# A macaron layer on one core: linear attention by 128-token tiles, the mixer's first products ahead of the last transposes, the result stored by column chunks

## The chip, the cores and the metric

The kernel runs on one core of one Trainium2 chip. Its engines work side by side, each through its own list of instructions in order: TensorE (PE in the rows) multiplies matrices, VectorE (DVE) and ScalarE (ACT) do elementwise work, GpSimd (POOL) does a little of it, and SyncE (SP) starts nearly all transfers between the chip's memory and the core's. An instruction that waits holds up everything behind it on its own engine. The metric is the device time of one execution in microseconds (us), the median over several; less is better. A matmul's weight load shows in the rows as an engine of its own, PEld.

## The reference

One decoder layer on 256 tokens of width 2048, in float32:

```python
h = h + 0.5 * swiglu(rmsnorm(h, ffn1_norm), ffn1_w_in, ffn1_w_out)      # inner width 5632
u = rmsnorm(h, mix_norm) @ w_in_mix       # pool input, q, k, v, output gate, gate's low rank (16)
y = concat(pool_mixer(u), gla_mixer(u))
h = h + y @ w_out_mix
h = h + 0.5 * swiglu(rmsnorm(h, ffn2_norm), ffn2_w_in, ffn2_w_out)
out = rmsnorm(h, final_norm)
```

The part `gla_mixer` is gated linear attention with 4 heads (keys of 128, values of 256), written in chunks of 64 tokens:

```python
b = cumsum(log_alpha) within a chunk           # log_alpha < 0, one per token and key column
q_dec, k_inv, k_tail = q * exp(b), k * exp(-b), k * exp(b_last - b)
o = (q_dec @ k_inv.T, kept where j <= i) @ v + q_dec @ state
state = state * exp(b_last) + k_tail.T @ v     # after each chunk
```

## The kernel before

**Tiles.** The 256 tokens are two tiles of 128 rows (`t` = 0 and 1; `h[0]` and `h[1]` show as `h_76` and `h_77` in listings). A product's columns go by chunks of `CW` = 512. Each float32 product is made of three passes in a rounded format (`three`, L162): high part by high part, high by low, low by high. ScalarE makes the high part of a weight block (`wh_...`, L108), VectorE the low part (`wl_...`, L109), in 14 buffers, that is seven pairs of high and low.

**Stages.** The order is FFN1 (`fi`, `fo`), mixer (`mgr`, `mk`, `mq`, `mv`, `mg`, `mp`, each a call of `project`), `w_out_mix` (`h`), FFN2 (`zi`, `zo`), final norm. The weights stream in through SyncE's queue, all in the order of their use. FFN products go by steps of two kinds listed in the table `OUT`: "S" is a plain step, "W" a step with fewer matmuls that first needs sums of weight blocks on VectorE and writes a second accumulator, `pw_...`.

**Accumulators.** The accumulator memory (PSUM) has 8 banks. In the FFNs two tags, `x` and `y`, of two two-bank buffers each hold a group's `ps_...` and `pw_...` in turn. In the mixer four banks (`ps_acc`) hold projections and four (`ps_t`) everything else. At each change of stage one set of pools closes and the next opens.

**FFN1's end.** `fo` is made for two column halves (`np_` = 0, 1). When a half is complete, `finish1` adds it to `h` (L561), sums squares (ScalarE) and transposes the new columns on TensorE (`transposed_rows`, 8 transposes `tp_h` for each chunk `n`, L367); ScalarE and VectorE turn each transposed tile into the high and low parts `h_hi`, `h_lo` (L286, L287), which are the moving operands of every mixer product. Chunks 0 and 1 are transposed in the middle of `np_` = 1, chunks 2 and 3 behind its last product. Then come the first halves (contraction over chunks 0 and 1) of `mgr` and `mk`, and then the second halves.

**Linear attention.** After q and k are projected, `bc` (L667) and `sf` (L676) are sums of the log decay by matmuls with a constant triangle, `sp` (L723) the scores of each 128-token tile (masked to 64-token blocks), `kv` (L744) the product of keys and values of each of the first three chunks, `st` the states (three, VectorE L749 and L754), `o` (L780, L785) the output: one matmul with the masked scores and, for each 64 rows behind the first chunk, one with a state.

**The end.** `finish2` adds the last half of `zo` to `h` (L915), finds the norm's factor `fin_r` (reduce and small steps on VectorE, a power on GpSimd L947, square sums on ScalarE), scales and stores the rows. GpSimd multiplies chunk 2 by the final gain (L924), VectorE does chunk 3 with gain and factor in two halves (L956) and scales chunks 1 and 2 by the factor (L966), ScalarE scales chunk 0.

The order on each engine is not written out by hand: a scheduler in the compiler's Tile layer sets it from the program's order, the buffers and its own costs.

## Time and profile before

| what | value |
|---|---|
| median of 3 runs | 1752.91 us (1752.67 to 1753.26) |
| the profiled execution | 1751.42 us |
| its span, first to last instruction | 1749.6 us |
| mean granted clock of TensorE | 0.996 |
| TensorE busy | 1726.8 us, 99% |
| VectorE busy | 1324.7 us, 76% |
| ScalarE busy | 912.3 us, 52% |
| weights and activations read | 334.56 MB |

The profile is one execution. Its span leaves 1.8 us of its time outside, and its time is 1.5 us under the median of the runs. Times in the rows count from the span's start. A row of the timeline gives the start, the time to the end of the last instruction that it merges, and in brackets how long the engine was idle before it and what ended that. Matmuls overlap, so one that shows 0.39 us may start 0.23 us after the one before; what a matmul costs is read from start to start. A plain float32 matmul shows as two records, one for each of its passes; a transpose shows as one.

### The profile page before, as it was taken

The numbers are of one execution on the slowest core, as the hardware profiler recorded it, in microseconds if no ns is written. First come the engines' busy times: TensorE is split into PE (matmuls) and PEld (weight loads), VectorE is DVE, ScalarE is ACT, GpSimd is POOL, SyncE is SP. The second block draws the span as 40 slices with busy tenths as digits, with TensorE's granted clock in tenths as the row PEclk, the third lists the DMA queues.
The fourth block names the chain that finished last, engine by engine and source line by source line (L and its number), as shares of the span: only waits on it lengthen the run. The fifth ranks groups of instructions, "written<-read, shape, count | busy, mean of one in ns | idle before, by whom it ended". The sixth has DMA issues, their size and how long they took to land.

```text
span 1749.6 us, 20543 instructions
## 1 busy us (share of the span) xinstructions
PE 1726.8 (99%) x7858; PEld 1428.2 (82%) x7858; DVE 1324.7 (76%) x1503; ACT 912.3 (52%) x1118; POOL 24.7 (1%) x26
## 2 busy tenths in 40 slices
PE   9999999999999999899999999999999999999997
PEld 6888888888888888788978888888888888888886
DVE  7978896878985878654555667878967788868788
ACT  8555544545544555464445554555545555545553
POOL 0000000000000000000000000000000000000002
PEclk9999999999999999999999999999999999999999
DMA  9564565655555655544554555654564645664652
GB/s 343 195 232 169 198 222 182 214 176 210 194 196 191 214 172 179 174 168 163 169 196 153 192 172 177 217 178 173 215 224 162 236 152 201 221 218 153 250 180 97
DMA packets 52052, 337.98 MB, mean 193 GB/s; under 512 B 5985, under 2 KB 9441, under 8 KB 13042
## 3 DMA queue, kind: packets, MB, share of 16 engines
q1 hardware_dynamic: 51522, 336.13, 55.0%
q8 instruction: 61, 1.00, 0.2%
q10 hardware_dynamic: 432, 0.55, 0.1%
q14 instruction: 37, 0.30, 0.0%
HBM read 334.56 MB, written 2.10 MB: 192 GB/s over the span
## 4 chain that ended last, share of the span: by engine, by line
PE 97%; DVE 1%; ACT 0%; DMA 0%; issue 0%; SPq 0%; POOL 0%; POOLq 0%; DVEq 0%; ACTq 0%
PE ps_zi L165 24%; PE ps_fi L165 23%; PE ps_zo L165 11%; PE ps_fo L165 11%; PE ps_h L165 5%; PE pw_fi L165 3%; PE pw_zi L165 3%; PE ps_mp L165 3%; PE ps_mv L165 2%; PE pw_fo L165 2%; PE pw_zo L165 2%; PE ps_mg L165 2%; PE ps_mk L165 1%; PE ps_mq L165 1%; PE ps_mgr L165 1%; PE ztp L441 1%
## 5 line engine op out<-in xcount | busy, mean ns | idle before, releaser
L109 DVE TENSOR_TENSOR wl_zi<-wr_zi,wh_zi 128x1024 fp32r<-128x1024 f32 (+1 forms) x216 | 250.6, 1173 | 106.7 <-ACT wh_zi L108 102.4
L108 ACT CAST wh_zi<-wr_zi 128x1024 fp32r<-128x1024 f32 (+1 forms) x216 | 215.7, 1012 | 217.9 <-PE ps_zi L165 150.8
L109 DVE TENSOR_TENSOR wl_fi<-wr_fi,wh_fi 128x1024 fp32r<-128x1024 f32 (+1 forms) x218 | 249.9, 1164 | 85.4 <-ACT wh_fi L108 81.1
L108 ACT CAST wh_fi<-wr_fi 128x1024 fp32r<-128x1024 f32 (+1 forms) x218 | 214.6, 1004 | 188.5 <-PE ps_fi L165 117.2
L165 PE MATMUL ps_fi<-wh_fi,xT_hi 128*128 128x512 f32 x584 | 226.8, 390 | 1.7 <-ACT wh_fi L108 1.7
L165 PE MATMUL ps_fi<-wl_fi,xT_hi 128*128 128x512 f32 x584 | 228.1, 391 | 0.1
L165 PE MATMUL ps_zi<-wl_zi,h_hi 128*128 128x512 f32 x584 | 228.0, 390 | 0.0
L165 PE MATMUL ps_zi<-wh_zi,h_hi 128*128 128x512 f32 x584 | 227.9, 390 | 0.0
L165 PE MATMUL ps_zi<-wh_zi,h_lo 128*128 128x512 f32 x584 | 227.6, 390 | 0.0
L165 PE MATMUL ps_fi<-wh_fi,xT_lo 128*128 128x512 f32 x584 | 226.4, 390 | 0.3 <-DVE xT_lo L287 0.3
L108 ACT CAST wh_fo<-wr_fo 128x1024 fp32r<-128x1024 f32 (+1 forms) x116 | 111.4, 999 | 94.3 <-DMA wr_fo<-in_ffn_w_out 35.1
L108 ACT CAST wh_zo<-wr_zo 128x1024 fp32r<-128x1024 f32 (+1 forms) x116 | 111.4, 998 | 92.7 <-DMA wr_zo<-in_ffn_w_out 34.1
L109 DVE TENSOR_TENSOR wl_fo<-wr_fo,wh_fo 128x1024 fp32r<-128x1024 f32 (+1 forms) x116 | 130.1, 1157 | 33.0 <-ACT wh_fo L108 32.7
L109 DVE TENSOR_TENSOR wl_zo<-wr_zo,wh_zo 128x1024 fp32r<-128x1024 f32 (+1 forms) x116 | 131.4, 1168 | 30.0 <-ACT wh_zo L108 25.2
L165 PEld LDWEIGHTS ps_fi<-wh_fi,xT_hi 128*128 128x128 f32 x584 | 109.5, 188 | 25.2 <-ACT wh_fi L108 2.8
L165 PEld LDWEIGHTS ps_fi<-wl_fi,xT_hi 128*128 128x128 f32 x584 | 109.6, 188 | 23.8 <-DVE wl_fi L109 1.4
L165 PEld LDWEIGHTS ps_fi<-wh_fi,xT_lo 128*128 128x128 f32 x584 | 109.6, 188 | 23.2 <-DVE xT_lo L287 0.7
L165 PEld LDWEIGHTS ps_zi<-wh_zi,h_lo 128*128 128x128 f32 x584 | 109.7, 188 | 22.5
L165 PEld LDWEIGHTS ps_zi<-wh_zi,h_hi 128*128 128x128 f32 x584 | 109.6, 188 | 22.5
L165 PEld LDWEIGHTS ps_zi<-wl_zi,h_hi 128*128 128x128 f32 x584 | 109.7, 188 | 22.3
L165 PE MATMUL ps_zo<-wl_zo,zhi 128*128 128x512 f32 (+1 forms) x272 | 105.2, 387 | 0.0
L165 PE MATMUL ps_zo<-wh_zo,zlo 128*128 128x512 f32 (+1 forms) x272 | 105.1, 386 | 0.0
(343 smaller groups left out, 3091.6 us busy)
## 6 DMA issues: line engine op xcount, KB each, us to landing
wr_zi<-in_ffn_w_in SPq DMA_DIRECT2D x88, 1024.0 KB, 4.9
wr_fi<-in_ffn_w_in SPq DMA_DIRECT2D x86, 1024.0 KB, 5.0
wr_fo<-in_ffn_w_out SPq DMA_DIRECT2D x44, 1024.0 KB, 5.1
wr_zo<-in_ffn_w_out SPq DMA_DIRECT2D x44, 1024.0 KB, 5.1
wr_h<-in_w_out_mix SPq DMA_DIRECT2D x16, 1024.0 KB, 5.0
wr_mv<-in_w_mv SPq DMA_DIRECT2D x8, 1024.0 KB, 4.9
wr_mp<-in_w_mp SPq DMA_DIRECT2D x8, 1024.0 KB, 4.9
wr_mg<-in_w_mg SPq DMA_DIRECT2D x8, 704.0 KB, 4.1
```

Of the source, the lines that this page charges most:

```text
L108: nc.scalar.copy(out=hi, in_=src)
L109: nc.vector.tensor_tensor(out=lo, in0=src, in1=hi.bitcast(F32), op=ALU.subtract)
L165: nc.tensor.matmul(ps, x, y, start=start and i == 0, stop=stop and i == 2, **kw)
L441: nc.tensor.transpose(tp[:, t, k, :], a_t[t][:, k * P : (k + 1) * P], ident)
```

## The change

- The `y` accumulators become a pool (`psy`) that lives through the whole kernel. `project` takes one two-bank pair of it in place of two single banks of `ps_acc`. FFN2 begins with `y`.
- `finish1` for the last half issues the first halves of `mgr` and `mk` between the updates of `h` and the last 16 transposes.
- In `OUT[3]`'s second list (the last slab of both FFNs' second products) the order S W S W S S becomes S S W W S S.
- Linear attention goes by tiles of 128 tokens. There is one state in place of three, so `sf`, `ktail`, `kv` and `st` are made for tile 0 alone, over 128 tokens; `o` takes the state only for tile 1, in one matmul of 128 rows. In return the scores between a tile's first and second 64 tokens (`sx`) are made, after VectorE has scaled the second half of `qdT`.
- At the end VectorE multiplies chunks 2 and 3 by gain and factor itself, GpSimd's two multiplications of the last half go, only tile 1 is worked in halves, and each chunk of 512 columns is stored by a transfer of its own (256 KB): chunks 2 and 3 on SyncE's queue, 0 and 1 on ScalarE's.

```diff
-        ((0, 0, "S"), (1, 0, "W"), (0, 1, "S"), (1, 1, "W"), (2, 0, "S"), (2, 1, "S")),
+        ((0, 0, "S"), (0, 1, "S"), (1, 0, "W"), (1, 1, "W"), (2, 0, "S"), (2, 1, "S")),
...
-        turn = [0]
+        turn = [0 if first else 1]
...
-    psum1 = ffn1.enter_context(tc.tile_pool(name="psum1", bufs=2, space=PSUM, reuse_waits="tile"))
+    psy = ctx.enter_context(tc.tile_pool(name="psy", bufs=2, space=PSUM))
+    psx1 = ffn1.enter_context(tc.tile_pool(name="psx1", bufs=2, space=PSUM, reuse_waits="tile"))
+    psum1 = {"x": psx1, "y": psy}
...
-            ps = [ps_acc.tile([P, CW], F32, tag="acc", name=f"ps_{name}_{t}") for t in range(NT)]
+            pair = psy.tile([P, NT, CW], F32, tag="y", name=f"ps_{name}")
+            ps = [pair[:, t, :] for t in range(NT)]
...
-    ps_r = project(hact, kd, io["w_mgr"], 336, "mgr", part=slice(0, KD // 2))
-    ps_k = project(hact, kd, io["w_mk"], CW, "mk", part=slice(0, KD // 2))
...
+        if np_ == 1:
+
+            for w, cw, wname in (("w_mgr", 336, "mgr"), ("w_mk", CW, "mk")):
+                early.append(project(hact, kd, io[w], cw, wname, part=slice(0, KD // 2)))
+        for n in range(2 * np_, 2 * np_ + 2):
+            s = slice(n * CW, (n + 1) * CW)
+            transposed_rows(
+                [h[t][:, s] for t in range(NT)], hT1[0][n], hT1[1][n],
+                [gains[:, 1, n * 4 + k : n * 4 + k + 1] for k in range(4)], f"h1{n}",
+                psx1 if grp.tags[0] == "x" else psy, grp.tags[0],
+            )
...
-    for t in range(NT):
-        sf = ps_t.tile([P, CW], F32, tag="tp", name=f"sf{t}")
-        nc.tensor.matmul(sf, tri[:, 1, :], la[:, t, :], start=True, stop=True)
-        nc.scalar.activation(out=Es[:, t, :], in_=sf, func=AF.Exp)
+    Es = gpool.tile([P, HEADS * DK], F32, tag="g_lo", name="Es")
+    sf = ps_t.tile([P, CW], F32, tag="tp", name="sf")
+    nc.tensor.matmul(sf, tri[:, 1, :], la[:, 0, :], start=True, stop=True)
+    nc.scalar.activation(out=Es, in_=sf, func=AF.Exp)
...
+    nc.gpsimd.tensor_tensor(out=ktail, in0=k_sb[:, 0, :], in1=Es, op=ALU.mult)
...
+    for t in range(NT):
+        first, second = slice(t * P, t * P + CHUNK), slice(t * P + CHUNK, (t + 1) * P)
+        nc.vector.tensor_tensor(
+            out=qdT[:, :, second], in0=qdT[:, :, second],
+            in1=E1[:, :, first.stop - 1 : first.stop].broadcast_to([P, HEADS, CHUNK]), op=ALU.mult,
+        )
+        sx = ps_t.tile([CHUNK, HEADS, CHUNK], F32, tag="tp", name=f"sx{t}")
+        for hh in range(HEADS):
+            nc.tensor.matmul(
+                sx[:, hh, :], kiT[:, hh, first], qdT[:, hh, second], start=True, stop=True
+            )
+        nc.vector.tensor_copy(sT[:CHUNK, t, :, CHUNK:], sx)
...
-    for n in range(3):
-        t, r = n // 2, slice((n % 2) * CHUNK, (n % 2 + 1) * CHUNK)
...
+    for hp in range(2):
+        kv = ps_t.tile([P, 2, DV], F32, tag="tp", name=f"kv{hp}")
+        for j in range(2):
+            hh = hp * 2 + j
+            nc.tensor.matmul(
+                kv[:, j, :], ktail[:, hh * DK : (hh + 1) * DK], v[0][:, hh * DV : (hh + 1) * DV],
+                start=True, stop=True,
+            )
+        nc.vector.tensor_copy(st[:, hp * 2 : hp * 2 + 2, :], kv)
...
-                for cc in range(2):
-                    n = 2 * t + cc
-                    if n == 0:
-                        continue
+                nc.tensor.matmul(o[:, j, :], sT[:, t, hh, :], vh, start=True, stop=t == 0)
+                if t == 1:
                     nc.tensor.matmul(
-                        o[cc * CHUNK : (cc + 1) * CHUNK, j, :],
-                        qdT[:, hh, n * CHUNK : (n + 1) * CHUNK], st[n - 1][:, hh, :],
-                        start=False, stop=True, skip_group_check=True,
+                        o[:, j, :], qdT[:, hh, P:], st[:, hh, :], start=False, stop=True
                     )
...
+        r = [factor(t, t == 1) for t in range(NT)]
+        for t in range(NT):
+            rows = slice(t * P, (t + 1) * P)
+            for n in (2, 0, 3, 1):
+                s = slice(n * CW, (n + 1) * CW)
+                if n < 2:
+                    nc.scalar.activation(out=h[t][:, s], in_=h[t][:, s], func=AF.Copy, scale=r[t])
+                    nc.scalar.dma_start(out=io["out"][rows, s], in_=h[t][:, s])
+                else:
+                    nc.vector.scalar_tensor_tensor(
+                        out=h[t][:, s], in0=h[t][:, s], scalar=r[t], in1=gf[n],
+                        op0=ALU.mult, op1=ALU.mult,
+                    )
                     nc.sync.dma_start(out=io["out"][rows, s], in_=h[t][:, s])
```

**TensorE at the end of FFN1.** A row of these listings has the source line, the operation, what is written and from what; buffer numbers are kept. Before, the sixteen transposes `tp_h` stand right behind the last matmul of `ps_fo`; these are the last four of them and what follows:

```order
L367 MATMUL tp_h_1_5597<-ident,h_76 128x128
L367 MATMUL tp_h_1_5597<-ident,h_77 128x128
L367 MATMUL tp_h_1_5597<-ident,h_76 128x128
L367 MATMUL tp_h_1_5597<-ident,h_77 128x128
L165 MATMUL ps_mgr_5634<-wh_mgr_0_5638,h_hi_114 128x336
L165 MATMUL ps_mgr_5634<-wl_mgr_0_5639,h_hi_114 128x336
L165 MATMUL ps_mgr_5634<-wh_mgr_0_5638,h_lo_118 128x336
```

In the changed kernel the first product of `ps_mgr` stands right behind the last of `ps_fo`:

```order
L165 MATMUL ps_fo_1_1_5329<-wh_fo_21_1_5509,fhi_5041 128x512
L165 MATMUL ps_fo_1_1_5329<-wl_fo_21_1_5510,fhi_5041 128x512
L165 MATMUL ps_fo_1_1_5329<-wh_fo_21_1_5509,flo_5042 128x512
L165 MATMUL ps_mgr<-wh_mgr_0_5576,h_hi_117 128x336
L165 MATMUL ps_mgr<-wl_mgr_0_5577,h_hi_117 128x336
L165 MATMUL ps_mgr<-wh_mgr_0_5576,h_lo_121 128x336
```

After 48 matmuls of `ps_mgr` and 48 of `ps_mk` come the first eight transposes, and the second halves begin at once, `h_hi_119` and `h_lo_123` being made from those transposes (the other eight stand four and four among the second halves):

```order
L165 MATMUL ps_mk<-wh_mk_1_5683,h_lo_122 128x512
L370 MATMUL tp_h_0_5711<-ident,h_76 128x128
L370 MATMUL tp_h_0_5711<-ident,h_77 128x128
L370 MATMUL tp_h_1_5720<-ident,h_76 128x128
L370 MATMUL tp_h_1_5720<-ident,h_77 128x128
L165 MATMUL ps_mgr<-wh_mgr_0_5780,h_hi_119 128x336
L165 MATMUL ps_mgr<-wl_mgr_0_5781,h_hi_119 128x336
L165 MATMUL ps_mk<-wh_mk_0_5894,h_hi_119 128x512
L165 MATMUL ps_mk<-wl_mk_0_5895,h_hi_119 128x512
L165 MATMUL ps_mgr<-wh_mgr_0_5780,h_lo_123 128x336
```

What moved is the whole first half of two projections, from behind the transposes to ahead of them.

**TensorE at the attention's output.** Before, the matmuls with the scores `sT` (128 rows) alternate with those with a state (64 rows each):

```order
L780 MATMUL o_0_6754<-v_6158,sT 128x256
L785 MATMUL o_0_6754<-st_6440,qdT 64x256
L780 MATMUL o_1_6763<-v_6158,sT 128x256
L785 MATMUL o_1_6763<-st_6440,qdT 64x256
L780 MATMUL o_0_6787<-v_6159,sT 128x256
L785 MATMUL o_0_6787<-st_6441,qdT 64x256
L785 MATMUL o_0_6787<-st_6442,qdT 64x256
L780 MATMUL o_1_6798<-v_6159,sT 128x256
L785 MATMUL o_1_6798<-st_6441,qdT 64x256
L785 MATMUL o_1_6798<-st_6442,qdT 64x256
```

Now every one has 128 rows, and tile 0 has none with a state:

```order
L791 MATMUL o_0_6735<-v_6165,sT 128x256
L791 MATMUL o_1_6742<-v_6165,sT 128x256
L791 MATMUL o_0_6764<-v_6166,sT 128x256
L793 MATMUL o_0_6764<-st,qdT 128x256
L791 MATMUL o_1_6773<-v_6166,sT 128x256
L793 MATMUL o_1_6773<-st,qdT 128x256
```

In both kernels two of the four heads stand together like this, and the others follow one matmul group at a time among the `ps_mp` products.

**VectorE at the end of the kernel.** Before, from tile 1's last update (`h_77`) on:

```order
L915 SCALAR_TENSOR_TENSOR h_77<-ps_zo_1_1_13047,h_77 128x256 x2
L948 SCALAR_TENSOR_TENSOR fin_v_13305<-fin_v_13305,fin_r_13307 128x1
L928 TENSOR_REDUCE pre_13322<-ss_h_7986 128x1
L951 SCALAR_TENSOR_TENSOR fin_r_13307<-fin_v_13305,fin_r_13307 128x1
L956 SCALAR_TENSOR_TENSOR h_76<-h_76,fin_r_13307,gf_12794 128x256 x2
L966 TENSOR_SCALAR h_76<-h_76,fin_r_13307 128x1024
L935 TENSOR_TENSOR pre_13322<-pre_13322 128x1
L938 TENSOR_SCALAR pre_13322<-pre_13322 128x1
L943 SCALAR_TENSOR_TENSOR fin_v_13332<-pre_13322 128x1
```

In the changed kernel, from the same place:

```order
L921 SCALAR_TENSOR_TENSOR h_77<-ps_zo_1_1_13013,h_77 128x256 x2
L962 SCALAR_TENSOR_TENSOR fin_r_13267<-fin_v_13258,fin_r_13267 128x1
L976 SCALAR_TENSOR_TENSOR h_76<-h_76,fin_r_13267,gf_12757 128x512
L976 SCALAR_TENSOR_TENSOR h_76<-h_76,fin_r_13267,gf_12760 128x512
L946 TENSOR_REDUCE pre_13271<-ss_h_7952 128x1
L950 TENSOR_SCALAR pre_13271<-pre_13271 128x1
L954 SCALAR_TENSOR_TENSOR fin_v_13272<-pre_13271 128x1
L959 SCALAR_TENSOR_TENSOR fin_v_13272<-fin_v_13272,fin_r_13285 128x1
L962 SCALAR_TENSOR_TENSOR fin_r_13285<-fin_v_13272,fin_r_13285 128x1
L976 SCALAR_TENSOR_TENSOR h_77<-h_77,fin_r_13285,gf_12757 128x512
L976 SCALAR_TENSOR_TENSOR h_77<-h_77,fin_r_13285,gf_12760 128x512
```

The scaling of tile 0 stands ahead of tile 1's factor in both, and the two stores of SyncE's queue for a tile now follow the two steps of L976.

## Rows read from the trace of the kernel before

**Rows 1.** The page: span, busy time of TensorE.
```profile
span 1749.6 us, 20543 instructions
PE 1726.8 (99%) x7858; PEld 1428.2 (82%) x7858; DVE 1324.7 (76%) x1503; ACT 912.3 (52%) x1118; POOL 24.7 (1%) x26
```

**Rows 2.** Timeline of TensorE, end of FFN1 to the second half of mgr.
```profile
718.16 0.28 PE L367 MATMUL tp_h<-ident,h 128*128 128x128 f32 x1
719.48 1.25 PE L367 MATMUL tp_h<-ident,h 128*128 128x128 f32 x7 [1.04 <-DVE h L561]
725.21 1.94 PE L367 MATMUL tp_h<-ident,h 128*128 128x128 f32 x8 [4.48 <-DVE h_lo L287]
...
745.76 0.39 PE L165 MATMUL ps_mk<-wh_mk,h_lo 128*128 128x512 f32 x1
745.99 0.31 PE L165 MATMUL ps_mgr<-wh_mgr,h_hi 128*128 128x336 f32 x1
...
747.38 0.32 PE L165 MATMUL ps_mgr<-wh_mgr,h_hi 128*128 128x336 f32 x1
```

**Rows 3.** Windows there: busy of PE, PEld, DVE, ACT, POOL, clock, DMA share, GB/s.
```profile
600.00:717.90 117.90, 115.92 (x525) 95.49 (x525) 93.38 (x111) 61.62 (x83) 0.00 (x0) 1.00 0.53 183
721.80:728.60 6.80, 3.39 (x14) 3.42 (x15) 5.64 (x15) 3.63 (x10) 0.71 (x1) 0.50 0.32 108
```

**Rows 4.** Timeline of ScalarE and VectorE behind the first transposes.
```profile
717.37 2.92 ACT L108 CAST wh_mk<-wr_mk 128x1024 fp32r<-128x1024 f32 x3
...
720.21 3.41 DVE L109 TENSOR_TENSOR wl_mk<-wr_mk,wh_mk 128x1024 fp32r<-128x1024 f32 x3
...
723.55 0.86 DVE L287 SCALAR_TENSOR_TENSOR h_lo<-tp_h,gains,h_hi 128x256 fp32r<-128x256 f32 x2
```

**Rows 5.** Timeline of TensorE in the middle of fo's last half.
```profile
702.99 1.04 PE L367 MATMUL tp_h<-ident,h 128*128 128x128 f32 x8
705.79 0.47 PE L165 MATMUL pw_fo<-wh_fo,fhi 128*128 128x512 f32 x1 [1.76 <-DVE h_lo L287]
```

**Rows 6.** Groups by line and shape, TensorE, the attention: count, busy us, mean ns.
```profile
L744 PE MATMUL kv<-v,ktail 64*128 64x256 f32 x24 | 5.4, 398 | 0.0
L785 PE MATMUL o<-st,qdT 128*64 128x256 f32 x24 | 5.2, 404 | 0.0
L780 PE MATMUL o<-v,sT 128*128 128x256 f32 x16 | 5.1, 398 | 0.0
L676 PE MATMUL sf<-la,tri 128*128 128x512 f32 x4 | 1.9, 593 | 0.0
```

**Rows 7.** Timeline of TensorE: the longest of four groups of kv.
```profile
842.61 2.00 PE L744 MATMUL kv<-v,ktail 64*128 64x256 f32 x12
```

**Rows 8.** Timeline of TensorE where FFN2 begins.
```profile
1030.40 0.39 PE L165 MATMUL ps_h<-wh_h,y_lo 128*128 128x512 f32 x1
...
1032.21 0.48 PE L165 MATMUL ps_zi<-wh_zi,h_hi 128*128 128x512 f32 x1
```

**Rows 9.** Timeline of all engines at the end.
```profile
1737.75 0.28 PE L165 MATMUL ps_zo<-wh_zo,zlo 128*128 128x256 f32 x1
...
1739.65 1.26 POOL L924 TENSOR_TENSOR h<-h,gf 128x512 f32<-128x512 f32 x1 [0.83 <-ACT sq_h L311]
1739.68 1.25 DVE L951 SCALAR_TENSOR_TENSOR fin_r<-fin_v,fin_r 128x1 f32<-128x1 f32 x1
...
1743.96 0.16 DVE L951 SCALAR_TENSOR_TENSOR fin_r<-fin_v,fin_r 128x1 f32<-128x1 f32 x1
1744.16 0.88 DVE L956 SCALAR_TENSOR_TENSOR h<-h,fin_r,gf 128x256 f32<-128x256 f32 x2
...
1745.77 0.33 SPq L968 DMA_DIRECT2D out<-h  x1
```

**Rows 10.** Issues of transfers: count, KB each, median us to landing.
```profile
out<-h SPq DMA_DIRECT2D x2, 640.0 KB, 3.0
out<-h ACTq DMA_DIRECT2D x2, 256.0 KB, 2.4
```

More of the change, by code (lines that the diff above doesn't have):

```diff
@@ L176, in __init__ @@
             self.acc = [
-                psum.tile([P, 2, CW], F32, tag=tags[0], name=f"ps_{name}_{t}") for t in range(NT)
+                psum[tags[0]].tile([P, 2, CW], F32, tag=tags[0], name=f"ps_{name}_{t}")
+                for t in range(NT)
             ]
@@ L511, in layer @@
     nc.vector.memset(zeros, 0.0)
-    idle = psum1.tile([P, CW], F32, tag="y", name="idle")
+    idle = psy.tile([P, CW], F32, tag="y", name="idle")
     for _ in range(8):
@@ L613, in layer, with finish1, block @@
     kd = list(range(KD))
-    ps_r = project(hact, kd, io["w_mgr"], 336, "mgr", part=slice(0, KD // 2))
-    ps_k = project(hact, kd, io["w_mk"], CW, "mk", part=slice(0, KD // 2))
+    hact = act_of(*hT1)
+    early = []
+    def finish1(np_, grp):
+        for i in range(2):
+            n = 2 * np_ + i
+            s = slice(n * CW, (n + 1) * CW)
+            for t in range(NT):
+                nc.vector.scalar_tensor_tensor(
+                    out=h[t][:, s], in0=grp.acc[t][:, i, :], scalar=0.5, in1=h[t][:, s],
+                    op0=ALU.mult, op1=ALU.add,
+                )
+                square_sum(h[t][:, s], ss1[:, t, n : n + 1], f"h1{t}{n}")
+        if np_ == 1:
[8 more added lines that the diff above has]
+            )
+    ffn(
+        psum1, spool1, x_act, lambda kp: x_s[kp], io["ffn1_w_in"], io["ffn1_w_out"], x_rows, "f",
+        finish1, first=True,
+    )
+    ffn1.close()
+    nc.sync.dma_start(out=pscale, in_=io["pscale"])
+    nc.sync.dma_start(out=gnorm, in_=io["gnorm"])
+    ps_r, ps_k = early
+    rstd = row_factor(ss1, "r_h1")
+    mixer = ExitStack()
+    ps_t = mixer.enter_context(tc.tile_pool(name="ps_t", bufs=4, space=PSUM, reuse_waits="tile"))
+    mix_sb = ExitStack()
+    mixc = mix_sb.enter_context(tc.tile_pool(name="mixc", bufs=1, reuse_waits="tile"))
+    blk = mix_sb.enter_context(tc.tile_pool(name="blk", bufs=MIX_BLOCKS, reuse_waits="tile"))
+    def block(shape, dtype, name):
+        return blk.tile(shape, dtype, tag="blk", name=name)
     tri = mixc.tile([P, 2, P], F32, name="tri")
@@ L734, in layer @@
             )
[L737 to L758 removed]
+    st = block([P, HEADS, DV], F32, "st")
+    for hp in range(2):
[5 more added lines that the diff above has]
+                start=True, stop=True,
+            )
+        nc.vector.tensor_copy(st[:, hp * 2 : hp * 2 + 2, :], kv)
     for c in range(2):
@@ L890, in layer @@
     mixer.close()
-    psum2 = ffn2.enter_context(tc.tile_pool(name="psum2", bufs=2, space=PSUM, reuse_waits="tile"))
+    psx2 = ffn2.enter_context(tc.tile_pool(name="psx2", bufs=2, space=PSUM, reuse_waits="tile"))
+    psum2 = {"x": psx2, "y": psy}
     gf = []
@@ L910, in finish2, with to_h @@
         half = CW // 2
-        for t in range(NT):
-            rows = slice(t * P, (t + 1) * P)
-            def to_h(s, src, ss):
+        def to_h(t, i, c, ss):
+            s = slice((2 * np_ + i) * CW + c.start, (2 * np_ + i) * CW + c.stop)
+            nc.vector.scalar_tensor_tensor(
+                out=h[t][:, s], in0=grp.acc[t][:, i, c], scalar=0.5, in1=h[t][:, s],
+                op0=ALU.mult, op1=ALU.add,
+            )
+            square_sum(h[t][:, s], ss, f"h3{t}{s.start}")
+        full = slice(0, CW)
@@ new lines, in finish2, with factor @@
+        if np_ == 0:
+            for t in range(NT):
+                for i in range(2):
+                    s = slice(i * CW, (i + 1) * CW)
+                    to_h(t, i, full, ss3[:, t, i : i + 1])
+                    nc.gpsimd.tensor_tensor(out=h[t][:, s], in0=h[t][:, s], in1=gf[i], op=ALU.mult)
+            return
+        def factor(t, halves):
+            pre = small.tile([P, 3], F32, tag="pre", name=f"pre{t}")
+            v = small.tile([P, 1], F32, tag="fv", name=f"fin_v{t}")
+            to_h(t, 0, full, ss3[:, t, 2:3])
+            if halves:
+                to_h(t, 1, slice(0, half), ss3[:, t, 3:4])
+                to_h(t, 1, slice(half, CW), pre[:, 1:2])
+            else:
+                to_h(t, 1, full, ss3[:, t, 3:4])
+            nc.vector.tensor_reduce(
+                out=pre[:, :1], in_=ss3[:, t, :], axis=mybir.AxisListType.X, op=ALU.add
+            )
+            d = pre[:, 2:] if halves else v
+            nc.vector.tensor_scalar(
+                out=d, in0=pre[:, :1], scalar1=1.0 / D, scalar2=EPS, op0=ALU.mult, op1=ALU.add
+            )
+            if halves:
@@ L942, in finish2 @@
-            v = small.tile([P, 1], F32, tag="fv", name=f"fin_v{t}")
-            nc.vector.scalar_tensor_tensor(
-                out=v, in0=pre[:, 2:], scalar=1.0 / D, in1=pre[:, :1], op0=ALU.mult, op1=ALU.add
-            )
             r = small.tile([P, 1], F32, tag="fr", name=f"fin_r{t}")
```

117 lines of the change are left out of this document (16 added, 101 removed).

## The prediction

> **What bounds the kernel now.** I read the page first: TensorE is busy 1726.8 of 1749.6 us [rows 1], so time is won only by taking work from TensorE, by closing one of its few gaps, or behind its last matmul. VectorE and ScalarE are not full, and matter only where TensorE waits for them. The second view is TensorE's timeline. Its largest gap lies between FFN1 and the mixer [rows 2]. The first transpose of chunks 2 and 3 starts at 718.16; seven more wait 1.04 us for the last update of `h`; the last eight wait 4.48 us, because they need the buffers of the first eight, and VectorE empties those only after it has made three low parts of `mk`'s weights, 3.41 us [rows 4]. The third view is the table of stretches: from 721.8 to 728.6 us TensorE's granted clock is 0.50, its lower level (1.2 GHz), behind that gap, while the 118 us before, which hold a wait of 1.76 us too [rows 3, 5], show 1.00. So the last eight transposes take 1.94 us against 1.25 for seven, and `mgr`'s first matmuls are slow too. From 718.16 the second half of `mgr` is reached at 745.99, 27.8 us later [rows 2].
>
> Two smaller gaps are like it. In the middle of `fo`'s last half, eight transposes at 702.99 are followed by a "W" matmul at 705.79 which waits for their tile to be emptied [rows 5]. And FFN2's first product starts at 1032.21, 1.8 us after the last matmul of `ps_h` starts at 1030.40 [rows 8]. In the attention, what counts is TensorE's own work [rows 6]. At the end the last matmul starts at 1737.75 and lasts 0.28 us, the last store is issued at 1745.77, and the span ends at 1749.6 [rows 1, 9].
>
> **Part 1, the first halves ahead of the transposes.** From 718.16 to the same point TensorE will do 48 matmuls of `mgr`, 48 of `mk` and 16 transposes of two passes. `mgr` costs 0.154 us a matmul (745.99 to 747.38 is nine) and `mk` 0.23 (745.76 to 745.99) [rows 2]: 7.4 + 10.9 us. A transpose at full clock costs 0.11 us (eight in 1.04 us, of which 0.16 is the overhang of the last record) [rows 5], sixteen 1.75. That is 20.1 us. New short waits come behind `mk`: on ScalarE the conversion of the first transposed tiles stands behind a cast of one block of `mk`'s weights, which needs a buffer that the last `mk` matmul frees, and casts cost 0.97 us (2.92 for three) [rows 4]; on VectorE the low parts stand behind the same block's low part, 1.14 us (3.41 for three) [rows 4]. TensorE can pass some of it with the eight transposes, some with the products that need the high part alone; I take 1.2 us. 27.8 − 21.3 is **−6.5**. The bounds: if no wait is covered, both blocks in a row (0.97 + 1.14) plus two conversions of 0.43 [rows 4] come on top of the 20.1, 23.1 in all, and −4.7; with no wait at all −7.7. Cover for the moved products: their moving operands come from chunks 0 and 1, whose last transposes ran at 702.99 [rows 5]; their weights are cast by 720.3 and split by 723.6 as things stand [rows 4], and `mk` starts 7.4 us behind 718.16, at 725.6. The new waits are each shorter than the 1.76 us of [rows 5], behind which the clock stayed full, so I expect no fall of the clock.
>
> **Part 2, the middle of `fo`.** With S S W W the "W" matmul comes 16 matmuls (3.6 us) behind the transposes, so the 2.8 us from 702.99 to 705.79 shrink to the transposes' own 0.9 [rows 5]: −1.9. But two "W" steps back to back need the second one's sums and splits from VectorE and ScalarE one after the other, and these stand behind the conversions of the same transposes; a cast and a low part as above are 1 us each [rows 4]. I take +1.0 and so **−0.9**, between −1.9 (all hidden) and +1 (three such steps in a row). FFN2's slab has the same new order without transposes; I cost it at nothing, because VectorE is a quarter idle [rows 1], and at +1.5 if that cover is missing.
>
> **Part 3, attention.** A pass over 256 columns costs 0.215 us: `sf` runs four passes of 512 columns in 1.9 us, of which 0.16 is the overhang of the last record [rows 6]. `kv` falls from 24 passes in four groups, 5.4 us [rows 6], to 8 in two: 1.7 + 2 × 0.16 = 2.0, and two switches between number formats (some 0.1 us each) go: −3.6. `o` falls from 40 passes, 10.3 us [rows 6], to 24 in the same five groups: 24 × 0.215 + 5 × 0.16 = 6.0; part of the old 10.3 is overhang counted in both rows, so −4.1. `sf` halves, −0.9. `sx` is new: 16 passes of 64 columns, for which no row exists. By columns alone they cost a quarter of 0.215 each, 0.9 us; at the cost of a transpose pass (0.109) 1.7; two switches add 0.2. I take 1.6, near the upper end, since so short a pass is nearer to the transposes. Sum **−7.0**, between −6.0 and −7.8. VectorE's new scalings of `qdT` and copies of `sx` (four steps of 256 columns, 0.43 each by the nearest row [rows 4]) are covered by the 23 `mv` matmuls between `sp` and `sx` (5.3 us); without that cover they would cost their 1.7.
>
> Here a rule speaks against the change. The Trainium skill, TensorEngine Tiling, Theoretical Speedup, says that matmuls with 64 rows can share the array and run up to twice as fast; then 24 half-filled `kv` passes would cost 2.6 us, not 5.4, and the part would bring 2.8 less. The trace shows a little of it: one group has 12 passes in 2.00 us [rows 7], 0.15 each, but the other 12 share the remaining 3.4 us, 0.28 each, so the sum goes by the row.
>
> **Part 4, FFN2's start.** The transposes move in among `zi`'s first 23 matmuls, which cover the wait for the last update of `h` (5.2 us at 0.23). 1.8 us less one matmul (0.23) and the eight transposes (0.87) leaves **−0.7**, and at worst 0.
>
> **Part 5, the end.** Now GpSimd's multiplication of tile 1 (1.26 us at 1739.65) runs beside a one-column step of VectorE that takes 1.25 us in place of 0.16 [rows 9]; the multiplication goes. In exchange VectorE does two steps of 512 columns for each tile (0.65 each, from 0.88 for two of 256, whose overlap makes 0.44 a half) where it had 0.88 + 0.75. I walked the listed order from the last matmul: update of `h_77` to 1739.7, tile 0's factor 1739.85, its two steps to 1741.15, tile 1's factor 1742.9 (0.4 us of steps, GpSimd's power 0.6, two more steps), its two steps to 1744.3. The last issue moves from 1745.77 to about 1744.6, −1.2, and the last transfer is 256 KB (2.4 us) in place of 640 (3.0) [rows 10], −0.6. Four transfers in flight share the bandwidth, so I take **−1.6**, between −0.5 and −2.4.
>
> **Sum.** −6.5 − 0.9 − 7.0 − 0.7 − 1.6 = −16.7 us. On the profiled execution that is 1751.42 to 1734.7, on its span 1749.6 to 1732.9. The median of the runs is 1.5 us above the profiled time, so I forecast 1736.2. With all bounds at their worst the parts give 4.7 − 1 − 1.5 + 6.0 + 0 + 0.5 = 8.7 saved (1744.2), at their best 7.7 + 1.9 + 7.8 + 0.7 + 2.4 = 20.5 (1732.4).
>
> **Rivals.**
> - The transposes' wait only moves behind `mk`: the last eight transposes again stand behind casts and low parts, a gap of some 4 us returns and the clock falls with it. For it: the conversions sit behind weight blocks on both engines in the changed order. Against it: products lie between the two groups of eight. Part 1 then brings about 2, and the time is 1740.7. Chance 0.13.
> - The end gives nothing, because tile 1's four stores share two queues: two transfers of 2.4 us in a row from 1743.8 would land at 1748.6 [rows 10], as late as now. The time is 1737.8. The Trainium skill, DMA: Bandwidth & Descriptors, Anatomy of one DMA, has a fixed cost of about 2 us for each transfer; 2.4 us for 256 KB and 3.0 for 640 [rows 10] agree that size adds little. Chance 0.12, and within my range.
> - Slower: the accumulator pairs. Each projection now needs a whole pair, and the pair comes free only when both its tiles are read, where single banks came free one by one. If nine projections each waited 2 us at their start (the size of the wait in [rows 5]), they would cost 18 us and the time would be 1754.2; it decides from 1.9 us a projection, and the kernel is slower by over 0.2% from 2.3. Against it: there are two pairs, and one full projection of 96 matmuls, 15 to 22 us, lies between the last write to a pair and its next use. Only `mq` is close, since `mgr` and `mk` finish together: it starts 23 matmuls (5.3 us) behind `mgr`'s last. Chance 0.03.
> - The attention's shorter work is eaten by waits for the new chain (scaling, `sx`, copy), so that of its 7.0 us only 2 remain: 1741.2. Against it are the 5.3 us of cover. Chance 0.05.
>
> **Chances and range.** The forecast with its parts inside their bounds has 0.67. From no change a measurement of this kernel tells apart about 0.2%, 3.5 us. Faster by more than that is every case but the third rival and a coincidence of several others: 0.94; within it 0.03; slower 0.03. The range 1731.5 to 1744.5 takes in the bounds and the rivals that are faster than before.
>
> **What would show it.** The wait of `tp_h` for `h_lo` is gone and no stretch near 722 us shows a clock of 0.50; the stretch from the last `ps_fo` to the last first-half product and 16 transposes takes about 21 us; `kv` has 8 passes and about 2 us, `o` about 6; `sx` 1 to 2; the last issue comes 6.5 us behind the last matmul, not 7.7. I am wrong if TensorE's waits name `h_hi` or `h_lo` behind `mk` for over 3 us, or name a new wait at a projection's start.

## The result and the profile after

The changed kernel takes 1734.82 us (median of 4 runs, 1734.08 to 1735.05) against 1752.79 of the kernel before beside it: a ratio of 0.9897, 95% interval 0.9880 to 0.9914. The forecast was 1736.2 in a range from 1731.5 to 1744.5. Repeated with other kernels it came out at 1734.56. The profiled execution has a span of 1733.05 us, 16.6 less than the 1749.64 of before [rows 1]; the forecast for the span was 1732.9.

The page: span, and busy times of the engines.

```profile
span 1733.1 us, 20485 instructions
PE 1717.8 (99%) x7840; PEld 1427.4 (82%) x7840; DVE 1316.3 (76%) x1493; ACT 911.1 (53%) x1117; POOL 24.9 (1%) x23
```

To see where the time came from, compare the start of the same TensorE instruction in both timelines. The lead of the changed kernel, in us, at the last matmul of a group (first differences are what each stretch brought):

| last matmul of | before | after | lead | the stretch brought |
|---|---|---|---|---|
| `ps_fi` (FFN1) | 649.95 | 650.56 | -0.61 | a later start, see below |
| `ps_fo` | 717.92 | 717.84 | 0.09 | 0.69: order of steps |
| `ps_mq` | 792.69 | 785.32 | 7.37 | 6.42 at the border, 0.86 by half of `sf` |
| `ps_mv` | 838.95 | 832.85 | 6.10 | -1.27: `sx` |
| `ps_mg` | 875.83 | 865.57 | 10.26 | 4.16: `kv` |
| `ps_mp` | 931.91 | 917.18 | 14.73 | 4.47: `o` |
| `ps_zo` | 1737.75 | 1722.24 | 15.51 | 0.78, of which 0.76 where FFN2 begins |
| end of the span | 1749.64 | 1733.05 | 16.59 | 1.08: the end |

The later start arises in the first 12 us, where both kernels do the same work: between 8 and 12 us TensorE has a granted clock of 0.57 and gets through 12 matmuls in the changed kernel's trace, and 1.00 and 18 in that of before. I count it as chance and not as the change, because experiment 1 below, with the pools of before, starts 0.3 us late as well. By this count the changed parts brought 17.2 us in these two traces, of which the span shows 16.6.

Timeline of TensorE between FFN1 and the mixer, in answer to [rows 2]:

```profile
717.84 0.39 PE L165 MATMUL ps_fo<-wh_fo,flo 128*128 128x512 f32 x1
718.06 0.31 PE L165 MATMUL ps_mgr<-wh_mgr,h_hi 128*128 128x336 f32 x1
...
736.34 1.04 PE L370 MATMUL tp_h<-ident,h 128*128 128x128 f32 x8
737.78 0.42 PE L165 MATMUL ps_mgr<-wh_mgr,h_hi 128*128 128x336 f32 x1 [0.40 <-ACT h_hi L289]
...
739.06 0.42 PE L165 MATMUL ps_mgr<-wh_mgr,h_lo 128*128 128x336 f32 x1 [0.24 <-DVE h_lo L290]
```

`mgr` starts 0.22 us behind the last `ps_fo`, an ordinary distance; the 4.48 us have become 0.40 and 0.24, behind the converted tiles, at the place where the prediction had put 1.2. The stretches answer to [rows 3]; the granted clock stays at 1.00, the upper level, with gaps of that size:

```profile
718.00:735.00 17.00, 17.00 (x92) 15.30 (x92) 12.18 (x20) 10.01 (x16) 0.70 (x1) 1.00 0.72 260
735.00:746.00 11.00, 10.36 (x61) 8.79 (x60) 6.38 (x10) 5.81 (x10) 0.00 (x0) 1.00 0.38 118
```

In the middle of `fo` (TensorE's timeline, [rows 5]) the wait of 1.76 us is gone, and with it one of 0.22 us for `wl_fo`; two new ones stand for the casts and splits of the second W step:

```profile
698.76 0.49 PE L165 MATMUL ps_fo<-wh_fo,fhi 128*128 128x512 f32 x1 [0.35 <-ACT wh_fo L108]
700.02 0.50 PE L165 MATMUL ps_fo<-wl_fo,fhi 128*128 128x512 f32 x1 [0.77 <-DVE wl_fo L109]
```

The attention by groups of line and shape, in answer to [rows 6]:

```profile
L791 PE MATMUL o<-v,sT 128*128 128x256 f32 x16 | 4.4, 378 | 0.0
L793 PE MATMUL o<-st,qdT 128*128 128x256 f32 x8 | 2.4, 379 | 0.0
L765 PE MATMUL kv<-v,ktail 128*128 128x256 f32 x8 | 2.1, 378 | 0.0
...
L745 PE MATMUL sx<-qdT,kiT 128*64 128x64 f32 x16 | 1.1, 225 | 0.0
L687 PE MATMUL sf<-la,tri 128*128 128x512 f32 x2 | 1.0, 594 | 0.0
```

`o` costs 6.8 us busy where it cost 10.3, `kv` 2.1 where it cost 5.4. A pass of `sx` (64 columns) takes 0.058 us from start to start, about a quarter of a pass of 256 columns (0.215). FFN2 begins without a gap [rows 8]: 1015.65 to 1015.88, one matmul.

```profile
1015.65 0.39 PE L165 MATMUL ps_h<-wh_h,y_lo 128*128 128x512 f32 x1
1015.88 0.39 PE L165 MATMUL ps_zi<-wh_zi,h_hi 128*128 128x512 f32 x1
```

The end, in answer to [rows 9]: all engines' timeline, the issues of tile 1's stores in pairs.

```profile
1722.24 0.28 PE L165 MATMUL ps_zo<-wh_zo,zlo 128*128 128x256 f32 x1
...
1727.01 0.16 DVE L962 SCALAR_TENSOR_TENSOR fin_r<-fin_v,fin_r 128x1 f32<-128x1 f32 x1
1727.20 1.41 DVE L976 SCALAR_TENSOR_TENSOR h<-h,fin_r,gf 128x512 f32<-128x512 f32 x2
...
1727.98 0.99 SPq L980 DMA_DIRECT2D out<-h  x2
1728.01 0.98 ACTq L974 DMA_DIRECT2D out<-h  x2
```

And the issues of stores by count, size and median us to landing [rows 10]:

```profile
out<-h SPq DMA_DIRECT2D x4, 256.0 KB, 2.7
out<-h ACTq DMA_DIRECT2D x4, 256.0 KB, 3.3
```

All stores together:

```profile
DMA to landing us min/median/max: 2.4/3.0/3.6
```

Tile 1's factor comes at 1727.01, 16.95 us earlier than before [rows 9], 1.4 more than the lead that was there already; the last issue ends 6.7 us behind the last matmul's start (it was 8.4). But 256 KB take longer to land than 2.4 us: the last two stores, one on each queue, land 3.3 and 3.6 us behind their issue, the last one of before (640 KB) 3.0. The last issue starts 1.6 us earlier behind the last matmul, the last landing comes 1.0 earlier, and the end 1.1.

### The profile page after: what moved, and what is told of

The parts are those of the page before. It is cut to its first block, busy times and chain, and to the rows that moved or that the text cites. A ratio compares the mean times of both kernels' runs of the same rounds, so it can differ in the third digit from the quotient of the medians.

```text
span 1733.1 us, 20485 instructions
## 1 busy us (share of the span) xinstructions
PE 1717.8 (99%) x7840; PEld 1427.4 (82%) x7840; DVE 1316.3 (76%) x1493; ACT 911.1 (53%) x1117; POOL 24.9 (1%) x23
## 4 chain that ended last, share of the span: by engine, by line
PE 97%; DMA 1%; ACT 1%; DVE 1%; issue 0%; SPq 0%; DVEq 0%; POOLq 0%; POOL 0%; ACTq 0%
PE ps_zi L165 24%; PE ps_fi L165 22%; PE ps_fo L165 11%; PE ps_zo L165 11%; PE ps_h L165 5%; PE pw_fi L165 3%; PE pw_zi L165 3%; PE ps_mp L165 3%; PE ps_mv L165 3%; PE pw_fo L165 2%; PE pw_zo L165 2%; PE ps_mg L165 2%; PE ps_mq L165 1%; PE ps_mk L165 1%; PE ps_mgr L165 1%; PE ftp L444 1%
## 5 line engine op out<-in xcount | busy, mean ns | idle before, releaser
L165 PE MATMUL ps_fo<-wl_fo,fhi 128*128 128x512 f32 x268 | 104.8, 391 | 0.8 <-DVE wl_fo L109 0.8
```

What stands on the lines that cost most here:

```text
L165: nc.tensor.matmul(ps, x, y, start=start and i == 0, stop=stop and i == 2, **kw)
```

## The experiments

Spans are those of the profiled execution; the kernel before ran beside each (medians 1752.46 to 1752.52). The start of FFN1 differs between executions: apart from experiments 9 and 11 the last `ps_fi` starts anywhere from 649.95 to 651.00. A difference of up to 1 us between two spans alone thus means little; where I give a smaller one it is read between two points of the timelines.

**1. Old pools.** The pools and `finish1` of before, all the rest as changed:

```diff
-    psy = ctx.enter_context(tc.tile_pool(name="psy", bufs=2, space=PSUM))
-    psx1 = ffn1.enter_context(tc.tile_pool(name="psx1", bufs=2, space=PSUM, reuse_waits="tile"))
+    psum1 = ffn1.enter_context(tc.tile_pool(name="psum1", bufs=2, space=PSUM, reuse_waits="tile"))
...
+    ps_acc = mixer.enter_context(tc.tile_pool(name="ps_acc", bufs=4, space=PSUM, reuse_waits="tile"))
```

> The changed kernel with the accumulator pools and finish1 of before (the first halves of mgr and mk are called behind finish1 again, projections take single banks, FFN2 begins with x); attention, end and the order S S W W stay. If the first halves ahead of the transposes bring what the traces of before and after show (6.4 us between FFN1 and the mixer's q) and FFN2's start 0.75, the span is 1733.1 + 7.1 = 1740.2 us, a wait of 4 to 5 us of tp_h for h_lo is back, and a stretch near 722 us has a granted clock of 0.50. If the gain there came from elsewhere (the attention, or the order of steps in fo), the span stays within 2 us of 1733.1.

Measured: 1742.20 us, ratio 0.9941 (0.9924 to 0.9957), span 1740.6. The gap is back in TensorE's timeline:

```profile
719.10 1.25 PE L367 MATMUL tp_h<-ident,h 128*128 128x128 f32 x7 [1.05 <-DVE h L561]
724.84 1.94 PE L367 MATMUL tp_h<-ident,h 128*128 128x128 f32 x8 [4.49 <-DVE h_lo L287]
```

And so is the low clock in the stretches behind it (the third number from the end):

```profile
722.00:729.00 7.00, 4.16 (x17) 4.19 (x18) 5.54 (x16) 3.13 (x8) 0.70 (x1) 0.59 0.29 98
729.00:740.00 11.00, 11.00 (x61) 10.23 (x60) 4.66 (x5) 4.07 (x5) 0.00 (x0) 0.95 0.57 191
```

From the last `ps_fo` to the last `ps_mq` it loses 7.3 us to the changed kernel, and 0.8 more where FFN2 begins. So the gain at both borders belongs to the pools and the calls together. Here `mgr`'s matmuls stay at 0.28 us, the lower level, until about 730; before they did until 728.6 behind the same gap, which is the most part of the difference between 7.3 and the 6.4 above.

**2. The calls written late again.** The lasting pool stays; in `finish1` the calls of the first halves go behind the transposes:

```diff
-        if np_ == 1:
-            for w, cw, wname in (("w_mgr", 336, "mgr"), ("w_mk", CW, "mk")):
-                early.append(project(...))
         for n in range(2 * np_, 2 * np_ + 2):
             transposed_rows(...)
+        if np_ == 1:
+            for w, cw, wname in (("w_mgr", 336, "mgr"), ("w_mk", CW, "mk")):
+                early.append(project(...))
```

> The changed kernel with one thing undone: in finish1 the calls of the first halves of mgr and mk are written behind the transposes, as before; the lasting pool of y accumulators stays. Theory 1, the order in the code does it: the gap comes back, span near 1739.5 us (+6.4), clock 0.50 near 722 us. Theory 2, the lasting pool does it: with a pair free the scheduler itself puts products of mgr ahead of the last transposes (its list shows 14 of them ahead of the first, and the transposes spread among the products), so that the 4.5 us wait stays away and the span is within 1.5 us of 1733.1.

Measured: 1733.96 us (1733.31 to 1734.11), ratio 0.9894 (0.9879 to 0.9908), span 1732.3. The scheduler has put `mgr` ahead of the transposes by itself and strewn them among the products; the rows are all the transposes that TensorE's timeline has there, and none has a wait:

```profile
720.37 0.27 PE L370 MATMUL tp_h<-ident,h 128*128 128x128 f32 x1
722.64 0.49 PE L370 MATMUL tp_h<-ident,h 128*128 128x128 f32 x3
723.27 0.60 PE L370 MATMUL tp_h<-ident,h 128*128 128x128 f32 x4
732.86 0.60 PE L370 MATMUL tp_h<-ident,h 128*128 128x128 f32 x4
733.77 0.60 PE L370 MATMUL tp_h<-ident,h 128*128 128x128 f32 x4
```

Theory 1 falls. The lasting pool, with the pairs that the projections take from it, makes the gain; writing the calls early loses 0.9 of it again (at the last `ps_mq` this kernel leads by 0.74 having been 0.16 behind at the last `ps_fo`), 0.64 of it by the two waits of 0.40 and 0.24. Where the rest lies was not traced; it is not the number of changes from products to transposes, since the transposes stand in five groups here and in three in the changed kernel.

**3. The pools alone.** The kernel before with the lasting pool only, the calls late. Beside the kernel before:

```diff
+    psy = ctx.enter_context(tc.tile_pool(name="psy", bufs=2, space=PSUM))
...
-            ps = [ps_acc.tile([P, CW], F32, tag="acc", name=f"ps_{name}_{t}") for t in range(NT)]
+            pair = psy.tile([P, NT, CW], F32, tag="y", name=f"ps_{name}")
+            ps = [pair[:, t, :] for t in range(NT)]
```

> The kernel before with one part of the change alone: the lasting pool of y accumulators (projections take pairs of it, FFN2 begins with y); calls behind the transposes, order of steps, attention and end are those of before. By the theory that the lasting pool does it, both gaps at the stage borders go: -7.1 (6.4 + 0.7) and the 0.6 that the code order left, so span 1749.6 - 7.7 = 1741.9 us. By the theory that the code order is needed, only FFN2's start moves: 1748.9.

Measured: 1742.48 us, ratio 0.9945 (0.9932 to 0.9959), span 1740.7: 8.9 us off the span by this part alone. 7.4 lie between the last `ps_fo` and the last `ps_mq`, 0.8 at FFN2's start, and 1.3 at `kv`; FFN1 started 0.6 later. The gain at `kv` I had not expected. `kv` is still made of 24 passes of 64 rows, but the scheduler has grouped them otherwise, 4, 16 and 4 in place of 4, 12, 4 and 4 (TensorE's timeline, the middle group):

```profile
837.21 2.11 PE L755 MATMUL kv<-v,ktail 64*128 64x256 f32 x16
```

**4. The attention by chunks again.** `sf`, `ktail`, `kv`, `st`, `o`, the triangle and the missing `sx` of before:

```diff
-    st = block([P, HEADS, DV], F32, "st")
+    st = [block([P, HEADS, DV], F32, f"st{n}") for n in range(1, 4)]
+    for n in range(3):
...
```

> The changed kernel with the attention by chunks of 64 tokens, as before. The trace of after gives kv -4.2, o -4.5, sf -0.9, sx +1.3 us on TensorE, so the span should be 1733.1 + 8.3 = 1741.4 us; by my prediction's sum 1740.1. If the attention's work were hidden behind other waits, within 2 us of 1733.1.

Measured: 1741.49 us, ratio 0.9937 (0.9923 to 0.9952), span 1739.7. Counted from the last `ps_fo` to the last `ps_mp` this kernel is 6.85 us slower than the changed one. So the change of the attention brings +0.45 by `sx` and half of `sf` together, -2.85 by `kv` and -4.45 by `o`. That is under the 8.3 that I expected here and near the prediction's 7.0, because `kv` in this kernel too has the groups of 4, 16 and 4. Of the 4.16 us in the table above 1.3 thus come from the pools' new order, and 2.85 from the attention's own change.

**5. `kv` in halves.** To see what a pass of 64 rows costs:

```diff
-                kv[:, j, :], ktail[:, hh * DK : (hh + 1) * DK], v[0][:, hh * DV : (hh + 1) * DV],
-                start=True, stop=True,
+            for i, r in enumerate((slice(0, CHUNK), slice(CHUNK, P))):
+                nc.tensor.matmul(
+                    kv[i][:, j, :], ktail[r, hh * DK : (hh + 1) * DK],
+                    v[0][r, hh * DV : (hh + 1) * DV], start=True, stop=True,
+                )
```

> The changed kernel with kv made by two matmuls of 64 rows (tokens 0 to 63 and 64 to 127, into different banks, summed on VectorE) in place of each one of 128: 16 passes of 256 columns in place of 8. If passes of 64 rows cost what full ones cost, kv takes 16 x 0.215 + 0.3 = 3.7 us in place of 2.1 and the span grows by 1.7. If two of them run side by side, 2.1 us and no change. My prediction's rows had both: 0.17 us a pass in the group of 12, 0.28 in the others.

Measured once: 1736.07 us, span 1734.3; between the last `ps_mv` and the last `ps_mg` 0.79 us more than the changed kernel. TensorE's timeline has the 16 passes in two groups of eight:

```profile
833.61 1.13 PE L766 MATMUL kv<-v,ktail 64*128 64x256 f32 x8
834.67 0.43 PE L165 MATMUL ps_mg<-wh_mg,h_hi 128*128 128x352 f32 x1
```

Eight passes that alternate between the two halves of the rows take 1.06 us from the first to what follows them. In the trace they start in pairs, the two of a pair 0.007 us apart and the pairs 0.216 us apart, and 0.216 is also the distance of two passes of 128 rows (0.215). The groups of four that all use one half, in experiments 3 and 4, take 1.06 us too: there single passes start 0.216 us apart. So passes of different halves run side by side, by a factor of two, and a pass of 64 rows without such a partner costs as much as a full one. Neither of the two expectations holds alone, because entering and leaving a group of 64 rows costs more than it does for full rows: 0.79 us for the two groups, 0.40 for each.

**6. The old order of steps.** The table's line of before:

```diff
-        ((0, 0, "S"), (0, 1, "S"), (1, 0, "W"), (1, 1, "W"), (2, 0, "S"), (2, 1, "S")),
+        ((0, 0, "S"), (1, 0, "W"), (0, 1, "S"), (1, 1, "W"), (2, 0, "S"), (2, 1, "S")),
```

> The changed kernel with the old order S W S W S S of the last slab's steps. My prediction's sum put the new order at -0.9 us (a wait of 1.8 us goes, some 1.0 of new ones comes); the traces show -0.7 in FFN1 and 0.0 in FFN2. So the span should be 1733.8 us, and the wait of pw_fo for h_lo of 1.8 us is back. If two W steps in a row cost what they save, 1733.1.

Measured: 1735.29 us (1735.10 to 1735.65) beside 1734.56 of the changed kernel on the same chip, span 1733.5. From the last `ps_fi` to the last `ps_fo` it is 0.69 us slower, and in FFN2 the same, as expected; the wait of `pw_fo` for `h_lo` is back with 1.76 us.

**7. The end of before.** `finish2` as it was, the rest as changed:

```diff
-        r = [factor(t, t == 1) for t in range(NT)]
...
+                nc.gpsimd.tensor_tensor(out=h[t][:, s], in0=h[t][:, s], in1=gf[n], op=ALU.mult)
...
+            c = slice(CW, 3 * CW + half)
+            nc.sync.dma_start(out=io["out"][rows, c], in_=h[t][:, c])
```

> The changed kernel with the end of before (GpSimd multiplies chunk 2, both tiles in halves, stores of 640, 256 and 128 KB). The traces give 1.1 us from the last matmul to the end, so the span should be 1734.2 us; by my prediction 1734.7. If the two layouts are equal to the chip and only the states differed, 1733.1.

Measured: 1735.48 us, ratio 0.9903 (0.9888 to 0.9918), span 1733.7; from the last matmul to the end 11.90 us where the changed kernel has 10.81, so the new end brings 1.09.

**8. Fewer stores for tile 0.**

```diff
-                    nc.scalar.dma_start(out=io["out"][rows, s], in_=h[t][:, s])
+                    if t == 1:
+                        nc.scalar.dma_start(out=io["out"][rows, s], in_=h[t][:, s])
```

> The changed kernel without the stores of tile 0's chunks 0 and 1 (512 KB of the result are not stored). If the end hangs on the rate at which all 2 MB go out, 512 KB at 380 GB/s are 1.4 us, of which tile 1's own steps, which come no earlier, leave something: the end comes 0.2 to 1 us earlier. If it hangs on tile 1's own 1 MB alone, nothing changes: 10.8 us from the last matmul's start to the end.

Measured once: span 1732.7; from the last matmul's start to the end 10.95 us, not less than 10.81. Stretches of the changed kernel at its end, and of this one (the last two columns are the share of the DMA engines and GB/s):

```profile
1725.90:1728.40 2.50, 0.00 (x0) 0.00 (x0) 1.74 (x5) 1.32 (x3) 0.56 (x1) 0.50 1.01 379
1728.40:1729.10 0.70, 0.00 (x0) 0.00 (x0) 0.21 (x1) 0.20 (x1) 0.00 (x0) 0.50 0.64 240
1729.10:1731.70 2.60, 0.00 (x0) 0.00 (x0) 0.00 (x0) 0.00 (x0) 0.00 (x0) 0.50 0.98 362
```

```profile
1726.50:1728.40 1.90, 0.00 (x0) 0.00 (x0) 1.59 (x4) 1.34 (x2) 0.00 (x0) 0.64 0.13 49
1728.40:1731.10 2.70, 0.00 (x0) 0.00 (x0) 0.00 (x0) 0.00 (x0) 0.00 (x0) 0.50 1.02 379
```

With half of tile 0's bytes gone the engines idle before 1728.4, but tile 1's 1 MB still takes 2.7 us at 379 GB/s. So the end of the changed kernel does not hang on these bytes of tile 0. It follows tile 1's first issue by 5.0 us before, 5.1 after, 5.2 here and 5.4 in experiment 9, where no half microsecond from 1734 to 1736 has a busy share under 0.98: there tile 0's bytes are still going out when tile 1's begin. That the first issue sets the end, within these 0.4 us, is read from four traces, and no run moves it alone.

**9. Tile 0's last scaling later**, on top of experiment 2:

```diff
+                nc.vector.scalar_tensor_tensor(
+                    out=r_late, in0=v, scalar=0.0, in1=r_0[0], op0=ALU.mult, op1=ALU.add
+                )
...
-                        out=h[t][:, s], in0=h[t][:, s], scalar=r[t], in1=gf[n],
+                        out=h[t][:, s], in0=h[t][:, s], scalar=r_late if (t, n) == (0, 3) else r[t],
+                        in1=gf[n],
```

> The calls of mgr and mk behind the transposes (the faster form), and at the end VectorE scales tile 0's chunk 3 behind tile 1's factor steps, while GpSimd makes the power, so that tile 1's first store is issued some 0.6 us earlier. If the end hangs on tile 1's first store (it came 5.0 and 5.1 us behind it in the two traces), the span is 1732.3 - 0.6 = 1731.7. If it hangs on the rate at which all 2 MB go out (380 GB/s from the first store of tile 0 on, with 0.27 us of pause), only some 0.3 us is to be had: 1732.0. If on neither, 1732.3.

Measured: 1741.71 us (1740.56 to 1742.06), ratio 0.9939 (0.9927 to 0.9952), span 1739.9. None of the expectations had this. The end moved the right way, by less than expected: tile 1's first store is issued 5.30 us behind the last matmul's start in place of 5.74, 0.44 earlier and not 0.6, and the end comes only 0.14 earlier. But TensorE lost 7.7 us in the FFNs, far from the edit, with the same 7840 matmul records in the same order and no new wait. It was not the chip: experiment 12 ran beside it at the changed kernel's usual time.

**10 and 11. Is it the place of the operands?** `r_late` is a new tile of 4 bytes in each partition. In the built program it moves the tiles that lie behind it by 64 bytes, among them what the FFNs' W steps work with: the sums that are their moving operands (`shi`, `slo` and the like) and half-sized weight blocks. Experiment 10 puts the value into a column that exists; 11 makes the new tile 64 bytes large, which moves them by 128.

```diff
-        r_late = small.tile([P, 1], F32, tag="rl", name="r_late")
+        r_late = []                                                              (10)
+                r_late.append(pre[:, :1])                                        (10)
+        r_late = small.tile([P, 16], F32, tag="rl", name="r_late")[:, :1]        (11)
```

> The same instructions as late_scale, but the copy of tile 0's factor goes into a column that exists already in place of a new tile, so that every tile lies where it lay in the kernel with the late calls. If late_scale's 7 us on TensorE came from the 64 bytes by which its new tile moved the operands of the FFNs, they go, and the span is 1732.3 - 0.15 = 1732.2 us. If they came from the changed order at the end, the span is 1739.9 again.

> late_scale with a new tile of 64 in place of 4 bytes, which moves the same operands by 128 bytes in place of 64. If what counts is the place of an operand within 128 bytes, the matmuls cost 0.227 us again and the span is 1732.2. If any move costs, or what counts is the place in something larger, the span stays near 1740.

Measured: 1733.83 us (1733.49 to 1734.42), ratio 0.9895 (0.9878 to 0.9911), span 1732.0, for 10; 1741.08 us, ratio 0.9936 (0.9916 to 0.9955), span 1738.9, for 11. One stretch, the same in four kernels, by the count of matmuls that TensorE got through (the number behind the second x is PEld's): first experiment 2, then 9, 11 and 10.

```profile
20.00:690.00 670.00, 669.86 (x2997) 554.39 (x2996) 545.12 (x600) 359.14 (x422) 0.71 (x1) 1.00 0.57 203
```

```profile
20.00:690.00 670.00, 669.98 (x2981) 551.31 (x2981) 542.76 (x595) 357.53 (x420) 0.71 (x1) 1.00 0.57 203
```

```profile
20.00:690.00 670.00, 670.00 (x2984) 552.09 (x2983) 542.64 (x596) 357.31 (x419) 0.71 (x1) 1.00 0.57 203
```

```profile
20.00:690.00 670.00, 669.59 (x2996) 554.24 (x2995) 545.09 (x600) 359.13 (x424) 0.71 (x1) 1.00 0.57 203
```

Thirteen to sixteen matmuls fewer in 670 us, at a full clock and fully busy. The trace also says which: one group of matmuls that read a moved sum, in experiment 2 and in 9 (count, busy us, mean ns):

```profile
L165 PE MATMUL pw_fi<-wl_fi,shi_x 128*128 128x512 f32 x60 | 23.4, 389 | 0.0
```

```profile
L165 PE MATMUL pw_fi<-wl_fi,shi_x 128*128 128x512 f32 x60 | 23.7, 395 | 0.0
```

The 816 FFN matmuls with a moved sum as their moving operand go from 0.228 to 0.234 us on average from start to start, which is 5.0 of the 7.7 us, and up to three matmuls behind each such stretch another 1.6; the 1488 of the mixer lose nothing. Experiment 11 shows the same (5.1 and 1.6 of 6.8). So the moved tiles cost it, the place within 128 bytes is not what decides, and which place would be good stays open.

**12. The changed kernel again**, beside 3, 6 and 9:

> The changed kernel once more, unaltered, beside the next three on one chip: a time of 1734.8 us within 0.5, span 1733.1 within 0.7. If the kernel with the late calls of mgr and mk is really the faster one (1734.0 in the runs before), this stays above it; if that was the chip, both come out at one time.

Measured: 1734.56 us (1733.93 to 1735.03), span 1733.2. The kernels of experiments 2 and 10 (1733.96 and 1733.83, measured beside others) lie below it by 0.6 and 0.7, and the timelines give 0.9; their ratios' intervals overlap with its own (0.9883 to 0.9913), so the times alone do not prove it.

## Why the prediction was right

The sum was -16.7 and the span moved by -16.6. That the two agree so closely is in part luck: the attention brought 1.2 more than its term, the end 0.5 less, and FFN1's later start took 0.6. The median moved by 18.0, to 1.4 us below the forecast; the forecast added 1.5 us to the profiled time, because the profiled execution of before was that much faster than its median, and the changed kernel's (1734.83) was not. By its parts:

- **Part 1** (-6.5) measured -6.4 in the trace. The size was right, and so was the mechanism on the chip: the wait for `h_lo` is covered and the clock keeps its upper level. The reason given was not: the prediction credits the calls that are written ahead of the transposes, and experiments 2 and 3 show that the lasting pool alone brings 7.4 and the early calls take 0.9 back. I had compared only the two finished orders, where both come together. The prediction's mechanism, products ahead of the transposes, is thus what happened; what puts them there was named wrongly. Its new waits were sized 1.2 and measured 0.64.
- **Part 2** (-0.9) measured -0.7, with 0.35 + 0.77 of new waits where 1.0 was taken; FFN2's slab cost nothing, as said.
- **Part 3** (-7.0): in the timelines of before and after it is 8.2, more than its upper bound of 7.8, and 6.85 when the attention's own change is undone. The difference of 1.3 is the pools' doing, since `kv`'s passes of 64 rows were grouped worse before. By terms of the timelines `kv` brought 4.16 (3.6 taken), `o` 4.47 (4.1), `sf` 0.86 (0.9), and `sx` cost 1.27 (1.6). The reason for the 1.6 was off: `sx` goes by columns, 0.93 us for 16 passes, and not near a transpose; the rest is its two switches. The prediction's 0.28 us for a pass of 64 rows counts the ends of three groups, while its 0.15 beside it leaves an end out; from start to start a pass without a partner costs 0.216. The Trainium skill, TensorEngine Tiling (Array Packing), Theoretical Speedup, gives up to twice the speed for 64 rows; experiment 5, where the halves alternate, agrees, with 0.216 us for two passes. In the trace of before only eight of the 24 passes started in pairs, so it was right to let the sum go by the rows.
- **Part 4** (-0.7) measured -0.76.
- **Part 5** (-1.6) measured -1.08. The step that was off is the term of -0.6 for a last transfer of 256 KB (2.4 us) in place of 640 (3.0). The last issue moved by 1.6 where 1.2 was taken, but the last stores took 3.3 and 3.6 us to land and not 2.4. From tile 1's first issue to its last landing the same 1 MB took 4.1 us in the three stores of before and 4.2 in the four of the changed kernel. So what counts is the first issue, which moved by 1.2, and not the size of the last store.

Of the rivals, the transposes' new gap is there, but 0.64 us long and without a fall of the clock; the rival that the end gives nothing did not come true, though it was right that four stores on two queues land later: 2.4 to 3.6 us for the same 256 KB. For a fixed cost it named the Trainium skill, DMA: Bandwidth & Descriptors, Anatomy of one DMA; that section is about transfers issued by GpSimd, and these were issued by SyncE and ScalarE, so the measured landings decide. No projection waits for its pair (TensorE's waits name none), and the chain with `sx` shows no wait.

## What to carry to other kernels

A stage border that closes one set of accumulators and opens the next can be an order that no one wrote: with the old pools no product of the mixer stood ahead of the last transposes, with the lasting one 14 did at once. Before moving calls by hand, let a part of the accumulators live across the border and read what order the scheduler then makes; and undo each of two edits that look like one, since only that tells which of them pays.

At the end of a kernel, price the last stores together, from the first issue to the last landing (4.1 and 4.2 us for 1 MB here), and not by the last store's own landing time. And after any edit that adds a tile, however small, look at the count of matmuls in a stretch far away from it.
